# Side jobs of the input projection's pair stage, split into steps that are counted in matrix products

## The chip, the core and the metric

The kernel runs on one core of one Trainium2 chip. TensorE (PE in the profile, its weight loads PEld) multiplies; VectorE (DVE), ScalarE (ACT) and GpSimd (POOL) compute on SBUF and PSUM; SyncE (SP) issues most of the DMAs, and GpSimd issues some. Each engine works through its own queue in order. The metric is the time of one execution in device microseconds (us), the median of several runs.

## The reference

One inference step of a hybrid layer, in float32, for a prompt of 1024 rows and a sample of 64 rows with cached keys, values and states:

```python
xn = _rmsnorm(x, p['norm_mix_w'])
proj = xn @ p['w_in']                       # 1024 wide in, z | xBC | dt | q | k | v | g_ssm | g_att out
z, xbc, dt_raw, q, k, v, gate_ssm, gate_att = jnp.split(proj, ...)
...                                         # conv, SSD scan over chunks of 64, gated norm
q = _partial_rope(_rmsnorm(q.reshape(b, t, 2 * ATT_HEADS, ATT_HEAD_DIM), p['q_norm_w']), q_pos)
k = _partial_rope(_rmsnorm(k.reshape(b, t, 2 * ATT_HEADS, ATT_HEAD_DIM), p['k_norm_w']), q_pos)
k_all = jnp.concatenate([k_past, k], axis=1)
o = _diff_attention(q, k_all, v_all, q_pos, k_pos, lam)
...
x = x + mix @ p['w_out']
...                                         # conv feed-forward
return x, k, v, ssm_new, conv_new, ffn_new  # the normed and rotated k is an output
```

## The kernel before

**Arithmetic.** A float32 number is held as two parts: `hi`, the number rounded to a shorter format (a copy on ACT), and `lo`, the rest (a subtraction on DVE). A product of two numbers is three matmuls (hi x hi, hi x lo, lo x hi), summed in PSUM. The 1088 columns (1024 + 64 rows of the input) lie in the free dimension.

**Stages.** A first stage (up to about 56 us) computes the dt columns and value tiles of the projection, then come the other value tiles with their normalisation, the pair stage (about 116 to 489 us), the attention and the scan with the gate tiles and the rest of the projection (to about 1080 us), the output matrices and the feed-forward part.

**The pair stage.** It projects z, q and k in the manner of Winograd and Strassen: a block of 256 rows of output is seven products of sums of weights and sums of the input. There are 16 blocks n = 0 to 15: four of q, four of k, eight of z (`INPUT`). Each of the seven products p = 0 to 6 is done for two column halves s, so a block has 14 products, and each is 12 matmuls of 128 x 272 columns on line L584 (`pile` inside `in_pair`). A product's sum is evicted from its PSUM bank as soon as it stands: p = 0 and p = 2 by ACT (L619, L629), p = 1 and 3 by DVE (`u`, L621, L623), p = 4, 5 and 6 by DVE (`pre`, L631). p = 2 goes on in the bank of p = 0, p = 3 in that of p = 1 and p = 6 in that of p = 4, once these have been read. An eviction may therefore come about three products late before a matmul has to wait for it.

**What runs beside the products.**
- The weights of the next block: a load of `w_f` (SP), sums on POOL (L502, L503, L527, L531), `hi` on ACT (L479) and `lo` on DVE (L489).
- When a block is done, its rows are stored to DRAM: z through a SiLU to `z_sc`, q and k to `q_r` and `k_r` (L612), with their squares summed in `ss`.
- The side jobs, in the iterator `beside`: `steps()` (8 turns), `cached_keys()` (8 parts of the cached keys, split into `hi` and `lo` and stored to `c_st`), and, after the four q blocks are done, `finishing("q")` and `finishing("k")`. Each of these has four idle turns, three statistics, then 12 parts (a fetch of 128 x 544 from `q_r` or `k_r` on POOL's queue, L726; a scale on DVE, L730; for k a store of the result to the output `kT`, L717, which the trace calls `out_dram`; `hi` on ACT, L410; `lo` on DVE, L411, in the place of x; two stores to `q_st` or `k_st`, L721), and four rotated parts (two fetches L738 and L739, the second of the `rope` table; the scale L744; the rotation L748 to L751; then the same stores).

The fetch and the rest of a part lie one turn apart (`in_turn`: it prepares the next item and finishes the one before), and a turn is given after every third product:

```python
u.send((p, s))
if s == 1:
    more_left(n + 1)
if at % 3 == 0:
    next(beside, None)
```

What is still left after the last block is run out by `run(beside)`. `seen["read"]` and `seen["copy"]` are the last eviction on DVE and ACT; a step recorded inside `tc.issue_after(...)` is not placed ahead of it. A list scheduler then sets each engine's order. Before, the jobs need 73 turns and the blocks give 74.

**Buffers.** The x of all jobs come from `fx` (three buffers of 128 x 1088 columns), `xh`, the rope rows `rp` and the rotation's product `rt` from `fc` (three). Weights come from the pool `wp` with tiles of 1088 columns, of which all but those of the first stage use 1024 or fewer.

**After the pair stage** the scores of the attention (`sc`, L986) need `q`, `kh` and `kl`, loaded from `q_st` and `k_st` on SP's queue (L914), and the gate tiles are plain products on L161 to L163.

Of the kernel before, what the change touches and what calls it, by code (L numbers as in the profile page):

```python
# [9 lines left out]
F32 = mybir.dt.float32  # L10
# [7 lines left out]
P = 128  # L18
# [42 lines left out]
RAW = 6  # L61
IN_ROWS = dict(fs=2, fu=2, fp=3, fc=3, fx=3, ss=2)
ZS = 4
# [26 lines left out]
def hybrid_layer(ctx: ExitStack, tc: tile.TileContext, xT, xt, prm, cst, rope, wvd, win, wbs, wba, wout, wup, wdn,  # L90
# [45 lines left out]

    wp = tc.alloc_tile_pool(name="wp", bufs=1, side="right")
    extra, turn, ahead, quick = None, 0, AHEAD_IN, QUICK

    def weight_tiles(k, m, pool=None):  # L140
        nonlocal turn
        if pool is None:
            turn = (turn + 1) % 3
        p, b = (pool, 1) if pool is not None else (extra, 1) if extra is not None and turn == 0 else (wp, 2)
        w = p.tile([P, WMAX], F32, name="w_f", tag="w_f", bufs=b)
        hi = p.tile([P, WMAX], R32, name="w_hi", tag="w_hi", bufs=b)
        lo = p.tile([P, WMAX], R32, name="w_lo", tag="w_lo", bufs=b)
        return [t[:, : k * m].rearrange("p (k m) -> p k m", k=k) for t in (w, hi, lo)]
# [248 lines left out]
    for u in range(2):  # L397
        w = wp.tile([P, WMAX], F32, name="w_f", tag="w_f", bufs=2)[:, :1024]
# [93 lines left out]
    def left_parts(blocks, early=None, by=G, order=(0, 1, 2, 3)):  # L492

        a = []
        for src in blocks:
            w = wp.tile([P, WMAX], F32, name="w_f", tag="w_f", bufs=2)
# [14 lines left out]
        def shared():  # L511
            t = [wp.tile([P, WMAX], R32, name=x, tag=x, bufs=2) for x in ("w_hi", "w_lo")]
# [18 lines left out]
        by.tensor_tensor(out=s2, in0=q12, in1=s2, op=ALU.subtract)  # L531
        hi, lo = (wp.tile([P, WMAX], R32, name=x, tag=x, bufs=2)[:, :n] for x in ("w_hi", "w_lo"))
        split_left(hi, lo, s2)
# [164 lines left out]

    def finishing(kind):
# [13 lines left out]

        def put(x, hi, j, n, c, w):
            rows_at = lambda y, r0: y[r0 + P * j : r0 + P * (j + n), c : c + w].rearrange("(j p) t -> p j t", p=P)
            if keep is not None:
                load(out=rows_at(keep, 0), in_=x)  # L717
            lo = x.bitcast(R32)
            split(hi, lo, x)
            for u, y in enumerate((hi, lo)):  # L720
                load(out=rows_at(to, D * u), in_=y.bitcast(F32))  # L721

        def part_of(j, c):
            def prepare():
                x = row("fx", "x")
                G.dma_start(out=x, in_=d[P * j : P * (j + 1), c : c + HT])  # L726
                return x,

            def finish(x):
                V.scalar_tensor_tensor(x, x, wcol(j), rs[:, c : c + HT], ALU.mult, ALU.mult)  # L730
                put(x.unsqueeze(1), row("fc", "xh", R32)[:, :HT].unsqueeze(1), j, 1, c, HT)

            return prepare, finish

        def turned(c):
            def prepare():
# [5 lines left out]
            def finish(x, cosine):  # L742
                for j in range(2):
# [7 lines left out]
                V.tensor_tensor(out=x[:, 1], in0=x[:, 1], in1=y[:, 0], op=ALU.add)  # L751
                put(x, couple(t.bitcast(R32)), 0, 2, c, QW)

            return prepare, finish

        yield from in_turn([part_of(j, c) for j in range(2, KT) for c in (0, HT)])
        for c in range(0, T, QW):
            yield from in_turn([turned(c)])

    def cached_keys():  # L760
        def part_of(j):
            def prepare():
                x = row("fx", "x")[:, :PAST]
                G.dma_start(out=x, in_=ckT[P * j : P * (j + 1), :])
                return x,

            def finish(x):
                hi = row("fc", "xh", R32)[:, :PAST]
                split(hi, x.bitcast(R32), x)
                for u, y in enumerate((hi, x)):  # L770
                    load(out=c_st[D * u + P * j : D * u + P * (j + 1), :], in_=y.bitcast(F32))

            return prepare, finish

        yield from in_turn([part_of(j) for j in range(KT)])

# [30 lines left out]
    while len(left[1]) < 7:  # L807
        more_left(1)
    beside = chain(steps(), cached_keys())
# [550 lines left out]
    def kept_weights(block, at):  # L1360

        w = wp.tile([P, WMAX], F32, name="w_f", tag="w_f", bufs=2)[:, :1024]
# [468 lines left out]
```

## Time and profile before

| | |
|---|---|
| median of 3 runs | 2460.97 us (2459.64 to 2466.04) |
| profiled execution, its own time | 2462.09 us |
| its span | 2460.3 us |
| mean granted clock of TensorE | 0.995 |
| TensorE busy | 2399.9 us (98%) |
| VectorE busy | 1752.4 us (71%) |
| ScalarE busy | 1223.4 us (50%) |
| GpSimd busy | 691.8 us (28%) |
| the pair stage | 116.4 to 489 us |

The profile is of one execution. A row of the timeline gives the start, the length, the engine, the line of the kernel, the instruction with its output and inputs, how many of them, and in brackets how long the engine was idle before it and what ended that wait. A row of a wait table gives the waiting engine and line, what it waited for, the time in total, the number of times and the longest. The granted clock is the share of full speed that TensorE was given.

### The profile page before, as it was taken

The page shows a single profiled execution, that of the slowest core. Times are in us where ns is not written, and L with a number is a line of the kernel's source. Part 1 is how long each engine was busy: PE and PEld are TensorE (multiplying, and loading weights), DVE is VectorE, ACT ScalarE, POOL GpSimd, SP SyncE. Part 2 cuts the span into 40 slices and gives each one's busy share as a digit, 9 for nine tenths or more (in the row PEclk, how much of TensorE's full clock was granted, in tenths as well). Part 3 has the DMA queues.
Part 4 walks back from the last instruction along what each step waited for, and adds up shares of the span by engine and source line. Part 5 has one row for each costly group of instructions (what it writes and reads, how often), then busy time and mean ns, then how long its engine had stood idle before and what let it go on. Part 6 is the DMA issues. An engine that isn't in the chain of part 4 may idle for free. (4 is left out here: it accounts for less than half of the span.)

```text
span 2460.3 us, 49370 instructions
## 1 busy us (share of the span) xinstructions
PE 2399.9 (98%) x18744; PEld 2322.8 (94%) x18744; DVE 1752.4 (71%) x3113; ACT 1223.4 (50%) x2706; POOL 691.8 (28%) x758
## 2 busy tenths in 40 slices
PE   8999999899999999999999999999999999999998
PEld 8999999899999999998899998999999999999998
DVE  4596885758687786865877665756977777787763
ACT  7354445346566565656655554434533333343441
POOL 0023233201011010114533331012254554535433
PEclk9999999999999999999999999999999999999999
DMA  7855666874554444345897954764124234268784
GB/s 254 277 169 184 224 209 215 280 211 139 164 155 139 131 146 148 108 135 190 277 329 253 332 183 149 214 204 155 55 91 172 91 123 169 80 237 232 197 216 77
DMA packets 283089, 449.79 MB, mean 183 GB/s; under 512 B 35610, under 2 KB 189347, under 8 KB 282851
## 3 DMA queue, kind: packets, MB, share of 16 engines
q1 hardware_dynamic: 271810, 420.30, 52.2%
q0 software_dynamic: 11040, 26.34, 5.5%
q8 instruction: 147, 2.41, 0.4%
q14 instruction: 92, 0.75, 0.1%
HBM read 294.03 MB, written 152.50 MB: 181 GB/s over the span
## 5 line engine op out<-in xcount | busy, mean ns | idle before, releaser
L161 PE MATMUL mm<-b,w_hi 128*128 128x272 f32 x1792 | 529.5, 296 | 3.8 <-ACT gt L847 1.9
L163 PE MATMUL mm<-b,w_lo 128*128 128x272 f32 x1792 | 523.4, 292 | 1.3 <-DVE w_lo L155 1.1
L162 PE MATMUL mm<-b,w_hi 128*128 128x272 f32 x1792 | 522.1, 291 | 0.0
L161 PEld LDWEIGHTS mm<-b,w_hi 128*128 128x128 f32 x1792 | 338.6, 189 | 9.9 <-issue 4.2
L163 PEld LDWEIGHTS mm<-b,w_lo 128*128 128x128 f32 x1792 | 338.1, 189 | 4.7 <-issue 2.2
L162 PEld LDWEIGHTS mm<-b,w_hi 128*128 128x128 f32 x1792 | 338.8, 189 | 3.2 <-issue 2.3
L876 DVE SCALAR_TENSOR_TENSOR cc<-pre,par,cc 128x272 f32<-128x272 f32 (+1 forms) x288 | 140.0, 490 | 15.7 <-ACT cc L874 12.8
L1492 PE MATMUL mx<-m,w_hi 128*128 128x272 f32 x760 | 146.5, 290 | 3.0 <-DVE hb L1528 1.8
L1492 PE MATMUL mx<-n,wh 128*128 128x272 f32 x1080 | 144.2, 288 | 1.9 <-ACT wh L479 1.0
L155 DVE TENSOR_TENSOR w_lo<-w_f,w_hi 128x1024 fp32r<-128x1024 f32 (+1 forms) x82 | 103.3, 1262 | 55.8 <-ACT w_hi L154 53.6
L864 POOL COPY pre<-pre 128x3 f32<-128x3 f32 x72 | 23.5, 327 | 417.7 <-DVE cc L878 194.7
L1492 PEld LDWEIGHTS mx<-n,wh 128*128 128x128 f32 x1080 | 138.5, 188 | 2.5 <-ACT wh L479 1.2
L479 ACT CAST w_hi<-ws 128x512 fp32r<-128x512 f32 (+1 forms) x100 | 61.0, 610 | 158.3 <-PE mx L1492 76.8
L1000 ACT ACTIVATE p_t<-sc,mx 128x512 f32<-128x512 f32 (+6 forms) x144 | 106.2, 740 | 66.4 <-DVE mx L991 32.2
L483 DVE TENSOR_TENSOR wh<-w_f,wh 128x512 fp32r<-128x512 f32 (+1 forms) x101 | 99.1, 982 | 35.1 <-ACT wh L479 35.0
L1492 PEld LDWEIGHTS mx<-m,w_hi 128*128 128x128 f32 x760 | 119.4, 188 | 4.0 <-DVE hb L1528 2.4
L154 ACT CAST w_hi<-w_f 128x1024 fp32r<-128x1024 f32 (+1 forms) x82 | 85.9, 1048 | 69.6 <-PE mm L162 46.6
L1509 POOL TENSOR_TENSOR hb<-hb,cc 128x64 f32<-128x64 f32 (+2 forms) x66 | 86.4, 1328 | 110.7 <-DVE hb L1530 52.3
L502 POOL TENSOR_TENSOR ws<-w_f 128x512 f32<-128x512 f32 (+1 forms) x46 | 61.3, 1333 | 193.9 <-DMA w_f<-in_win_dram 114.2
L479 ACT CAST wh<-w_f 128x512 fp32r<-128x512 f32 (+1 forms) x144 | 88.1, 614 | 44.8 <-POOL pre L1523 15.4
L1492 PE MATMUL mx<-m,w_lo 128*128 128x272 f32 x380 | 109.8, 289 | 0.0
L1172 ACT ACTIVATE bc<-bc,nacum 128x128 f32<-128x128 f32 (+1 forms) x288 | 87.3, 383 | 15.7 <-POOL bc L1170 15.5
(452 smaller groups left out, 6974.8 us busy)
## 6 DMA issues: line engine op xcount, KB each, us to landing
w_f<-in_win_dram SPq DMA_DIRECT2D x78, 512.0 KB, 4.3
w_f<-in_wup_dram SPq DMA_DIRECT2D x45, 512.0 KB, 3.5
bc<-a_sc SPq DMA_DIRECT2D x32, 512.0 KB, 5.8
h_sc<-hb SPq DMA_DIRECT2D x44, 272.0 KB, 2.1
ht<-h_sc SPq DMA_DIRECT2D x22, 544.0 KB, 5.2
t_sc<-ht SPq DMA_DIRECT2D x22, 544.0 KB, 3.5
out_dram<-yq POOLq DMA_DIRECT2D x44, 272.0 KB, 5.8
x_sc<-cc SPq DMA_DIRECT2D x72, 136.0 KB, 2.4
```

The source lines that it names most:

```text
L154: S.copy(hi, w)
L155: V.tensor_tensor(out=lo, in0=w, in1=hi, op=ALU.subtract)
L161: PE.matmul(ps, a_hi, b_hi, start=i == 0, stop=False)
L162: PE.matmul(ps, a_hi, b_lo, start=False, stop=False)
L163: PE.matmul(ps, a_lo, b_hi, start=False, stop=i == n - 1)
L479: S.copy(hi, src)
L483: V.tensor_tensor(out=lo, in0=src, in1=hi, op=ALU.subtract)
L876: V.scalar_tensor_tensor(cc[:, :m], pre[:, i : i + m], cw(i), cc[:, :m], ALU.mult, ALU.add)
L1000: act(p_t[:n, :nk], sc[c][:n, :nk], AF.Exp, bias=mx[:n, c : c + 1], accum_out=dst)
L1172: act(bc[:L, e, :L], bc[:L, e, :L], AF.Exp, bias=nacum[:L, ch, 8 * g + e : 8 * g + e + 1])
L1492: PE.matmul(ps, w[x][:, c], b[y][:, k], start=start and k == i == 0, stop=k == 3 and i == 2, skip_group_check=not start)
L1509: G.tensor_tensor(out=hb[h][:, o : o + n], in0=hb[h][:, o : o + n], in1=cc[:, d : d + n], op=ALU.mult)
```

## The change

It touches the side jobs of the pair stage and two sizes.

- `in_turn` goes. A part is now a generator `job` in steps, and each step says how many products later the next one comes: fetch; 3 products; scale (and for k the store to `kT`); 1 product; `hi` on ACT and its store; 2 products, or 3 where there is a store to `kT`; `lo` on DVE and its store. `take_turn(at)` is called after every product, advances the jobs that run, and begins a new one after every third product.
- A rotated part takes one such start (before, two turns: the iterator of each held one item). The jobs now need 62 starts of the 74.
- `fx` has four buffers for x (before, three).
- The weight pool is closed after the first stage and opened again with tiles of 1024 columns (before, one pool of 1088).

```diff
-IN_ROWS = dict(fs=2, fu=2, fp=3, fc=3, fx=3, ss=2)
+IN_ROWS = dict(fs=2, fu=2, fp=3, fc=3, fx=4, ss=2)
...
+    wp.release()
+    wp, wide = tc.alloc_tile_pool(name="wp", bufs=1, side="right"), 4 * 256
...
-    def in_turn(items):
-
-        due = []
-        for prepare, finish in chain(items, [(None, None)]):
-            if prepare is not None:
-                due.append((finish, prepare()))
-            if len(due) > 1 or prepare is None and due:
-                finish, x = due.pop(0)
-                with tc.issue_after(seen["read"].ins):
-                    finish(*x)
-            yield
+    def job(fetch, scale, hi_of, hi_rows, lo_rows, keep=None):
+
+        x = fetch()
+        yield 3
+        hi = lambda: None
+        if scale is not None:
+            with after("read"):
+                x = scale(x)
+            if keep is not None:
+                load(out=keep, in_=x)
+            yield 1
+        with after("copy"):
+            hi = hi_of()
+            S.copy(hi, x)
+        load(out=hi_rows, in_=hi.bitcast(F32))
+        yield 2 if keep is None else 3
+        with after("read"):
+            V.tensor_tensor(out=x.bitcast(R32), in0=x, in1=hi, op=ALU.subtract)
+        load(out=lo_rows, in_=x)
+
+    running = []
+
+    def take_turn(at):
+        for x in list(running):
+            x[0] -= 1
+            if x[0] <= 0:
+                x[0] = next(x[1], None)
+                if x[0] is None:
+                    running.remove(x)
+        if at % 3 == 0:
+            new = next(beside, False)
+            if new:
+                running.append([next(new), new])
+            return new is not False or running
...
-            if at % 3 == 0:
-                next(beside, None)
+            take_turn(at)
...
-    run(beside)
+    while take_turn(0):
+        for _ in range(2):
+            take_turn(1)
```

The line numbers move: the products stand on L586, the evictions on L621, L623, L625, L631 and L633, the weights' `lo` on L491, the fetches of a part on L755, its scale on L759, its `kT` store on L708, `hi` and its store on L713, `lo` on L716 and its store on L717; a rotated part has its fetches on L771 and L772, its scale on L779 and the rotation on L783 to L786.

VectorE's queue, k parts beside the block that starts with `u_5137` (the numbers behind u mark the block): the scale, the subtraction and the evictions, before.

```order
L411 TENSOR_TENSOR x<-x,xh 128x544
L621 TENSOR_TENSOR u_5137<-mx,u_5136 128x272
L730 SCALAR_TENSOR_TENSOR x<-x,par,ss 128x544
L621 TENSOR_TENSOR u_5137<-mx,u_5136 128x272
L489 TENSOR_TENSOR wh<-w_f,wh 128x512
L730 SCALAR_TENSOR_TENSOR x<-x,par,ss 128x544
L411 TENSOR_TENSOR x<-x,xh 128x544
L623 TENSOR_TENSOR u_5136<-mx,u_5136 128x272
```

There the subtraction L411 of a part comes within an eviction or two of its scale L730. The same kind of place now, from the eviction of p = 3 on:

```order
L759 SCALAR_TENSOR_TENSOR x<-x,par,ss 128x544
L716 TENSOR_TENSOR x<-x,xh 128x544
L625 TENSOR_TENSOR u_4911<-mx,u_4911 128x272
L491 TENSOR_TENSOR wh<-ws_4948,wh 128x512
L625 TENSOR_TENSOR u_4911<-mx,u_4911 128x272
L491 TENSOR_TENSOR wh<-w_f,wh 128x512
L716 TENSOR_TENSOR x<-x,xh 128x544
L633 TENSOR_TENSOR pre<-mx,u_4911 128x272
L759 SCALAR_TENSOR_TENSOR x<-x,par,ss 128x544
```

The L716 directly behind an L759 belongs to the part before; the part of that L759 is subtracted at the next L716, behind two evictions and two weight splits.

VectorE's queue at the q rotations, now: from the second eviction of p = 3 (`u`) on, behind the scale of the first rotation.

```order
L625 TENSOR_TENSOR u_3801<-mx,u_3801 128x272
L491 TENSOR_TENSOR wh<-w_f,wh 128x512
L783 TENSOR_TENSOR rt<-x,rp 128x544
L633 TENSOR_TENSOR pre<-mm,u_3801 128x272
L784 TENSOR_TENSOR x<-x,rp 128x544
L633 TENSOR_TENSOR pre<-mm,u_3801 128x272
L491 TENSOR_TENSOR wh<-w_f,wh 128x512
L779 SCALAR_TENSOR_TENSOR x<-x,wq_1552,ss 128x272 x2
L785 TENSOR_TENSOR x<-x,rt 128x272
L786 TENSOR_TENSOR x<-x,rt 128x272
L633 TENSOR_TENSOR pre<-mx,u_3801 128x272
L783 TENSOR_TENSOR rt<-x,rp 128x544
```

Before, the same block has the beginning of one rotation, between the evictions of p = 6:

```order
L631 TENSOR_TENSOR pre<-mm,u_3791 128x272 x2
L489 TENSOR_TENSOR wh<-w_f,wh 128x512
L631 TENSOR_TENSOR pre<-mx,u_3791 128x272 x2
L489 TENSOR_TENSOR w_lo<-ws_3833,w_hi 128x512
L631 TENSOR_TENSOR pre<-mm,u_3792 128x272
L744 SCALAR_TENSOR_TENSOR x<-x,wq_1548,ss 128x272 x2
L748 TENSOR_TENSOR rt<-x,rp 128x544
L631 TENSOR_TENSOR pre<-mm,u_3792 128x272
```

The rotations of q begin earlier in the block and stand closer.

TensorE's queue at the end of the pair stage, before:

```order
L584 MATMUL mm<-b_1598,w_hi 128x272
L584 MATMUL mm<-b_1597,w_lo 128x272
L986 MATMUL sc<-kh_6145,q_6143 128x512
L986 MATMUL sc<-kh_6145,q_6143 128x128
L161 MATMUL mm<-b_916,w_hi 128x272
```

and now, the last product's end and, 48 matmuls of L161 to L163 later, the first scores:

```order
L586 MATMUL mm<-b_1602,w_hi 128x272
L586 MATMUL mm<-b_1601,w_lo 128x272
L161 MATMUL mm<-b_920,w_hi 128x272
L162 MATMUL mm<-b_921,w_hi 128x272
L163 MATMUL mm<-b_920,w_lo 128x272
```

```order
L161 MATMUL mm<-b_926,w_hi 128x272
L162 MATMUL mm<-b_927,w_hi 128x272
L163 MATMUL mm<-b_926,w_lo 128x272
L1021 MATMUL sc<-kh_6149,q_6147 128x512
L1022 MATMUL sc<-kl_6152,q_6147 128x512
```

Two products of a gate tile have moved ahead of the first scores.

More of the change, by code (lines that the diff above doesn't have):

```diff
@@ L511, in shared @@
         def shared():
-            t = [wp.tile([P, WMAX], R32, name=x, tag=x, bufs=2) for x in ("w_hi", "w_lo")]
+            t = [wp.tile([P, wide], R32, name=x, tag=x, bufs=2) for x in ("w_hi", "w_lo")]
             for i, src in enumerate((s1, q22)):
@@ L531, in left_parts @@
         by.tensor_tensor(out=s2, in0=q12, in1=s2, op=ALU.subtract)
-        hi, lo = (wp.tile([P, WMAX], R32, name=x, tag=x, bufs=2)[:, :n] for x in ("w_hi", "w_lo"))
+        hi, lo = (wp.tile([P, wide], R32, name=x, tag=x, bufs=2)[:, :n] for x in ("w_hi", "w_lo"))
         split_left(hi, lo, s2)
@@ L712, in finishing, with rows_at, part, fetch @@
             yield
[L714 to L724, printed above, removed]
+        def rows_at(y, r0, j, n, c, w):
+            return y[r0 + P * j : r0 + P * (j + n), c : c + w].rearrange("(j p) t -> p j t", p=P)
+        def part(j, c):
+            def fetch():
                 x = row("fx", "x")
                 G.dma_start(out=x, in_=d[P * j : P * (j + 1), c : c + HT])
[L727 to L729 removed]
+                return x
+            def scale(x):
                 V.scalar_tensor_tensor(x, x, wcol(j), rs[:, c : c + HT], ALU.mult, ALU.mult)
[L731 to L733 removed]
+                return x.unsqueeze(1)
+            at = j, 1, c, HT
+            return job(fetch, scale, lambda: row("fc", "xh", R32)[:, :HT].unsqueeze(1), rows_at(to, 0, *at), rows_at(to, D, *at),
+                       None if keep is None else rows_at(keep, 0, *at))
         def turned(c):
[L736 removed]
+            t = None
+            def fetch():
                 x, cosine = couple(row("fx", "x")), couple(row("fc", "rp"))
@@ L751, in finish, with part, fetch @@
                 V.tensor_tensor(out=x[:, 1], in0=x[:, 1], in1=y[:, 0], op=ALU.add)
-                put(x, couple(t.bitcast(R32)), 0, 2, c, QW)
-            return prepare, finish
-        yield from in_turn([part_of(j, c) for j in range(2, KT) for c in (0, HT)])
+                return x
+            at = 0, 2, c, QW
+            return job(fetch, scale, lambda: couple(t.bitcast(R32)), rows_at(to, 0, *at), rows_at(to, D, *at),
+                       None if keep is None else rows_at(keep, 0, *at))
+        for j in range(2, KT):
+            for c in (0, HT):
+                yield part(j, c)
         for c in range(0, T, QW):
-            yield from in_turn([turned(c)])
+            yield turned(c)
     def cached_keys():
-        def part_of(j):
-            def prepare():
+        def part(j):
+            def fetch():
                 x = row("fx", "x")[:, :PAST]
                 G.dma_start(out=x, in_=ckT[P * j : P * (j + 1), :])
[L765 to L775, printed above, removed]
+                return x
+            return job(fetch, None, lambda: row("fc", "xh", R32)[:, :PAST], *(c_st[D * u + P * j : D * u + P * (j + 1), :] for u in range(2)))
+        for j in range(KT):
+            yield part(j)
     def begun_in(n):
@@ L808, in hybrid_layer @@
         more_left(1)
-    beside = chain(steps(), cached_keys())
+    beside = chain(one_by_one(steps()), cached_keys())
     for n in range(1, len(INPUT)):
```

26 lines of the change are left out of this document (18 added, 8 removed).

## The prediction

> **What bounds the kernel now.** I read the page first, then the busy time by windows, the engine's own waits, and TensorE's timeline where it has a gap. The page says that TensorE is nearly the whole of the time:
>
> ```profile
> span 2460.3 us, 49370 instructions
> PE 2399.9 (98%) x18744; PEld 2322.8 (94%) x18744; DVE 1752.4 (71%) x3113; ACT 1223.4 (50%) x2706; POOL 691.8 (28%) x758
> ```
>
> Only 2460.3 - 2399.9 = 60 us are idle on PE. A change that leaves the matmuls alone can win part of that, and what PE loses by running at a lower clock. By windows (after each pair of times: length, PE busy; the number behind the POOL column is PE's granted clock, then the DMA share):
>
> ```profile
> 400.00:489.00 89.00, 78.16 (x596) 76.48 (x594) 62.79 (x106) 36.41 (x66) 26.02 (x28) 0.98 0.83 275
> 520.00:1080.00 560.00, 560.00 (x4317) 538.41 (x4316) 435.54 (x1028) 349.88 (x944) 57.17 (x163) 1.00 0.47 141
> ```
>
> The 560 us after the pair stage have no idle at all. The stretch 400 to 489, where the k parts run beside the products, has 89.00 - 78.16 = 10.8 us. TensorE's timeline shows the gaps (start, length, instruction, and in brackets the idle time before it with its releaser). The first two rows here are undisturbed: one starts 3.01 us after the other, so 12 matmuls, one product, take 1.505 us.
>
> ```profile
> 298.65 3.18 PE L584 MATMUL mx<-b,wh 128*128 128x272 f32 x24
> 301.66 3.19 PE L584 MATMUL mx<-t,wh 128*128 128x272 f32 x24
> 306.88 4.80 PE L584 MATMUL mx<-b,wh 128*128 128x272 f32 x24 [2.03 <-ACT u L619]
> ...
> 402.05 1.78 PE L584 MATMUL mx<-t,wh 128*128 128x272 f32 x12 [1.13 <-DVE u L621]
> 411.17 0.52 PE L584 MATMUL mx<-b,w_hi 128*128 128x272 f32 x2 [1.30 <-DVE pre L631]
> 426.27 1.77 PE L584 MATMUL mx<-t,wh 128*128 128x272 f32 x12 [1.20 <-DVE u L621]
> 435.69 0.52 PE L584 MATMUL mx<-b,w_hi 128*128 128x272 f32 x2 [1.60 <-DVE pre L631]
> 481.62 0.82 PE L584 MATMUL mm<-b,w_hi 128*128 128x272 f32 x2 [2.27 <-DVE pre L631]
> 489.11 0.87 PE L986 MATMUL sc<-kh,q 128*128 128x512 f32 x2 [2.80 <-ACT w_hi L154]
> 490.38 0.56 PE L161 MATMUL mm<-b,w_hi 128*128 128x272 f32 x1 [0.40 <-DVE pre L631]
> 494.14 0.43 PE L162 MATMUL mm<-b,w_hi 128*128 128x272 f32 x1
> 494.37 0.43 PE L163 MATMUL mm<-b,w_lo 128*128 128x272 f32 x1
> ```
>
> In each of these PE waits for an eviction of a product sum, so the question is what held the evicting engine. VectorE's waits answer it (in order: total us, times, longest):
>
> ```profile
> DVE x L411 <- DMA out_dram<-x: 16.8, 10, 3.8
> DVE x L730 <- DMA x<-k_r: 7.8, 4, 2.8
> ```
>
> The largest is self-made. For a k part the scaled x is stored to the output (out_dram), and the subtraction that overwrites x (L411) stands right behind in VectorE's queue, so VectorE sits until the store has read x. The eviction L621 stands behind that in its queue, and PE's gap at 402.05 ends with it:
>
> ```profile
> 399.83 1.82 DVE L411 TENSOR_TENSOR x<-x,xh 128x544 fp32r<-128x544 f32 x1 [3.84 <-DMA out_dram<-x]
> ```
>
> **The change, part by part.** *The k parts.* The subtraction now comes 1 + 3 = 4 products after the scale, 4 x 1.505 = 6.0 us. The store takes
>
> ```profile
> out_dram<-x SPq DMA_DIRECT2D x16, 272.0 KB, 3.7
> x<-k_r POOLq DMA_DIRECT2D x16, 272.0 KB, 4.3
> ```
>
> 3.7 us from issue, so it is covered with 2.3 us over. The gaps at 402.05, 411.17 and 435.69 (1.13 + 1.30 + 1.60 = 4.0 us) go whole. The wait for x<-k_r does not go: a part is still fetched three products, 4.5 us, ahead, a fetch takes 4.3 us, and it is issued from POOL's queue behind the weight sums. The fourth x buffer only lets that issue be punctual. I leave half of the gap at 426.27 in place: 0.6 of 1.20 us goes. The last gap, 2.27 us at 481.62, stands where the last rotations ran into the last block; the new steps end about two blocks earlier, so it goes, with its slow matmuls of the next 3 us (13 of them at about 0.23 us, the spacing of the last two rows, instead of 0.125: 1.3 us). I take 0.6 us off for what comes in its place. Sum: -4.0 - 0.6 - 2.3 - 1.3 + 0.6 = -7.6; I use -7.5.
>
> *The end of the stage.* Before, the last rotations of k lie in the last block, and their stores stand in SP's queue before and among the loads of the scores, the next user of TensorE:
>
> ```profile
> 483.55 1.54 SPq L914 DMA_DIRECT2D kh<-k_st  x2
> ```
>
> The scores' loads were issued at 483.55 to 485.09, and PE, which had nothing else in its queue, stood until 489.11: 2.80 + 0.40 = 3.2 us. Behind it about 26 matmuls ran at 494.37 - 494.14 = 0.23 instead of 0.125 us, 2.6 us more. Now PE has two products of a gate tile (48 matmuls, 6.0 us) before the first score, which covers the 4 us that the loads took, and no k store is left in the queue. Of 5.8 us I take -5.0; 0.8 stays for the first gate matmul, which may wait for an eviction (0.40 before).
>
> [...] The gaps of 2.03, 2.27 and 2.80 us were each followed by slow matmuls (24 in 4.80 us at 306.88, against 3.18), those of 1.1 to 1.6 us by none. So I count a clock cost for gaps of over 2 us, here 1.3 + 2.6, and 1.6 for 306.88. [...]
>
> *Cached keys and q parts.* The cached keys have one gap, and the q parts a second one beside that at 306.88:
>
> ```profile
> 218.58 1.77 PE L584 MATMUL mm<-b,wh 128*128 128x272 f32 x12 [1.26 <-ACT u L619]
> 295.52 0.51 PE L584 MATMUL mx<-b,w_hi 128*128 128x272 f32 x2 [0.70 <-DVE pre L631]
> ```
>
> ACT stood there for a key fetch that POOL issued late, behind a store from the third buffer; with four it should be earlier: -1.0 of 1.26. The q parts have no kept store; theirs are the gaps of 0.70 and 2.03 with the slow 24 matmuls (1.6 us), in all 4.3. They come with POOL's sums and with fetches that wait for a buffer. I count -3.0.
>
> *The rotated parts* are the new load. One takes on VectorE:
>
> ```profile
> 486.22 0.91 DVE L744 SCALAR_TENSOR_TENSOR x<-x,par,ss 128x272 f32<-128x272 f32 x2 [3.95 <-DMA x<-k_r]
> 488.03 0.71 DVE L748 TENSOR_TENSOR rt<-x,rp 128x544 f32<-128x544 f32 x1
> 490.15 0.71 DVE L749 TENSOR_TENSOR x<-x,rp 128x544 f32<-128x544 f32 x1
> 492.62 0.43 DVE L751 TENSOR_TENSOR x<-x,rt 128x272 f32<-128x272 f32 x1
> 496.10 0.72 DVE L411 TENSOR_TENSOR x<-x,rt 128x544 fp32r<-128x544 f32 x1 [3.05 <-DMA out_dram<-x]
> ```
>
> 0.91 + 0.71 + 0.71 + 0.43 + 0.43 + 0.72 = 3.9 us (L750 and L751 are alike). It had six products (9.0 us) and now has three (4.5 us). Evictions and weight splits (six in a block of 14 products) go beside it:
>
> ```profile
> 465.49 0.43 DVE L631 TENSOR_TENSOR pre<-mm,u 128x272 f32<-128x272 f32 x1
> 465.84 0.68 DVE L489 TENSOR_TENSOR w_lo<-w_f,w_hi 128x512 fp32r<-128x512 f32 x1
> ```
>
> Five of seven products are evicted by VectorE: 3 x 5/7 x 0.43 = 0.9 us, and 3 x 6/14 x 0.68 = 0.9 us of splits in three products: 5.7 us of work in 4.5, so VectorE falls 1.2 us behind per turn and 4.7 us in four. An eviction may be three products, 4.5 us, late before PE waits for its bank. So four bare rotations just fit; a fetch that lands late does not. I take +2.0 for the q rotations (bounds 0 and the 2.27 of one gap plus 2.03 of another, 4.3), and nothing for the k rotations beyond the 0.6 above.
>
> *The early stage.* Since the weight pool is closed and opened again after the first stage, the loads of the third and fourth value tiles wait for that stage's last product (55.8 us), and were free to go at 31.55 us. They are needed three value products later:
>
> ```profile
> 55.78 0.29 PE L161 MATMUL mx<-w_hi,xn_hi 128*128 128x272 f32 x1
> 64.83 0.28 PE L161 MATMUL mm<-w_hi,xn_hi 128*128 128x256 f32 x1
> 56.40 1.03 ACT L154 CAST w_hi<-w_f 128x1024 fp32r<-128x1024 f32 x1
> 57.47 1.23 DVE L155 TENSOR_TENSOR w_lo<-w_f,w_hi 128x1024 fp32r<-128x1024 f32 x1 [0.55 <-ACT w_hi L154]
> w_f<-in_win_dram SPq DMA_DIRECT2D x78, 512.0 KB, 4.3
> ```
>
> 64.83 - 55.78 = 9.05 us of cover against 4.3 + 1.03 + 1.23 = 6.6 us for one and about 1 more for the second: 0 if the loads go at once, up to 3 if they queue. I take +0.5. The narrower tiles change no instruction's size. In the other 1940 us only neighbours swap in the order; I allow 4 us either way and count 0.
>
> Sum: -7.5 - 5.0 - 1.0 - 3.0 + 2.0 + 0.5 = -14.0. The profiled execution took 2462.09 us (span 2460.3 and 1.8 around it), 1.1 above the median of 2460.97. 2460.97 - 14 = **2447 us**. A measurement of this kernel can tell about 0.3%, 7.4 us, from no change.
>
> **The rivals.**
> 1. *The stalls move.* VectorE waits 7.8 us for x<-k_r at L730, and the lead of the fetch is unchanged; what the subtraction no longer waits for, the scale might. For it: 4.3 us landing against 4.5 of lead. Against: the largest gaps followed the store's wait. Then only the end's idle time is won (-3 to -5), less the rotations (+2): about -3, 2458.
> 2. *Slower: the crowded rotations.* Place: the eight turns with a rotation. The slack left is nil after four bare ones, so it decides when VectorE waits over 3.3 us in a turn (4.5 - 1.2); it did wait 3.95 for x<-k_r at 486.22 and PE lost 2.27. Neighbours of POOL's sums are longer as well:
>
> ```profile
> 262.50 3.68 DVE L730 SCALAR_TENSOR_TENSOR x<-x,wq,ss 128x544 f32<-128x544 f32 x1
> 263.05 1.29 POOL L503 TENSOR_TENSOR ws<-ws,w_f 128x512 f32<-128x512 f32 x1
> 403.25 0.77 DVE L730 SCALAR_TENSOR_TENSOR x<-x,par,ss 128x544 f32<-128x544 f32 x1
> ```
>
> 3.68 beside POOL's sums, 0.77 without. If every turn loses 2.27 (18 us) and half of them the clock (4 x 1.5 = 6), that is +24 in place of the +2.0, and the sum is -16 + 24 = +8: 2469. Against it: the block of 14 products, 21.1 us, has room for 10 evictions (4.3), six splits (4.1) and the 2.7 rotations that fall into it (10.5), together 18.9. [...]
> 3. *The early gap.* If the reloads queue behind one another, PE loses 3 us and 2 of clock: 2447 + 5 = 2452.
> 4. *All of it goes.* No rotation cost and all gaps with their clock (7.5 + 1.3, 5.8, 1.3, 4.3): -20, 2441.
>
> **How the numbers follow.** Forecast 0.55, stalls move 0.17, slower 0.15, early gap 0.06, all goes 0.07. The range leaves out most of the slower case and a little below: 2440 to 2463. Faster by over 0.3%: the forecast, all goes and the early gap, less 0.01 for the forecast's own tail (its range is 2442 to 2455), 0.67; same: the stalls that move and that tail, 0.18; slower 0.15.
>
> **What would show it.** Right: no wait of VectorE's subtraction for out_dram above 1 us; the 400-to-489 stretch some 7 us shorter; gate matmuls directly after the last product and no gap before the first score; the k stores over two blocks before the end. Wrong: gaps of over 2 us in blocks with rotations, waits on rp<-in_rope_dram or x<-k_r longer than 3.3 us, a gap near 64.8 us, or a busy sum of PE that differs by more than the clock explains.

## The result and the profile after

The changed kernel takes 2455.86 us (median of 10 runs, 2448.28 to 2458.71) against 2463.07 us before (median of 10, 2458.10 to 2466.04). The ratio is 0.9971, 95% interval 0.9959 to 0.9982: 7.2 us faster. The forecast was 14 us faster; the sign was right, the size half. The profiled execution took 2457.46 us, 1.6 above its median, so the two traces differ by only 4.6 of the 7.2 us:

```profile
span 2455.7 us, 49366 instructions
PE 2398.2 (98%) x18744; PEld 2323.0 (95%) x18744; DVE 1738.6 (71%) x3113; ACT 1225.4 (50%) x2707; POOL 694.8 (28%) x758
```

TensorE's timeline, all gaps of over 1 us from the pair stage to 520 us (start, length, instruction, idle time before it and its releaser):

```profile
125.96 0.52 PE L586 MATMUL mx<-b,w_hi 128*128 128x272 f32 x2 [2.70 <-ACT u L621]
150.50 0.52 PE L586 MATMUL mm<-t,w_hi 128*128 128x272 f32 x2 [1.32 <-DVE pre L633]
296.43 0.52 PE L586 MATMUL mx<-b,w_hi 128*128 128x272 f32 x2 [1.31 <-DVE pre L633]
320.84 0.52 PE L586 MATMUL mm<-b,w_hi 128*128 128x272 f32 x2 [2.97 <-DVE pre L633]
345.46 0.51 PE L586 MATMUL mm<-b,w_hi 128*128 128x272 f32 x2 [2.82 <-DVE pre L633]
393.86 0.59 PE L586 MATMUL mx<-b,w_hi 128*128 128x272 f32 x2 [2.01 <-DVE pre L633]
427.65 2.58 PE L586 MATMUL mm<-b,wh 128*128 128x272 f32 x12 [1.79 <-ACT u L621]
515.42 0.44 PE L1021 MATMUL sc<-kh,q 128*128 128x384 f32 x1 [2.56 <-ACT p_t L1035]
```

The gap of 1.26 us at the cached keys and the 3.2 us ahead of the first scores are gone, and the five k gaps of before have become two. New are 2.97 and 2.82 us beside the q rotations, 1.9 us more at the start, and 2.56 us at 515, behind the gate products that were moved forward. The points at which the two traces can be laid side by side are the fifth product (123.55 before, 125.96 after), the last matmul of the pair stage (486.0 and 487.0) and the last score, whose start ends the ranges here, before and then after:

```profile
L986 PE MATMUL sc<-kh,q x208: 191/338/765, 489.1 to 1073.1; 128*128 128x512 f32 x73, 128*128 128x384 f32 x8, 128*128 128x256 f32 x8, 128*64 128x64 f32 x8
```

```profile
L1021 PE MATMUL sc<-kh,q x208: 191/338/506, 493.2 to 1070.6; 128*128 128x512 f32 x73, 128*128 128x384 f32 x8, 128*128 128x256 f32 x8, 128*64 128x64 f32 x8
```

So the start lost 2.4 us, the rest of the pair stage won 1.4 (362.4 to 361.0), the end of the stage won 3.5 (587.1 to 583.6), and the stretch behind it won 2.1 (1387.2 to 1385.1), a stretch that takes 1381.5 to 1392.0 us in the traces of all the kernels here. VectorE's waits of the side jobs over the stage:

```profile
DVE x L759 <- DMA x<-k_r: 9.8, 3, 4.2
DVE x L716 <- DMA out_dram<-x: 7.7, 7, 1.7
DVE x L759 <- DMA x<-q_r: 5.3, 3, 2.9
DVE rt L783 <- DMA rp<-in_rope_dram: 2.2, 2, 1.6
```

The wait for the kT store, 16.8 us before, is 7.7, none longer than 1.7. The wait of the scale for fetched k rows, 7.8 us before, is 9.8. One of them in VectorE's timeline, and POOL's queue ahead of an earlier one of 3.54 us (at 391.09):

```profile
424.63 0.78 DVE L759 SCALAR_TENSOR_TENSOR x<-x,par,ss 128x544 f32<-128x544 f32 x1 [4.21 <-DMA x<-k_r]
```

```profile
382.05 1.50 POOL L504 TENSOR_TENSOR ws<-w_f 128x512 f32<-128x512 f32 x1 [10.66 <-DMA w_f<-in_win_dram]
383.63 1.28 POOL L505 TENSOR_TENSOR ws<-ws,w_f 128x512 f32<-128x512 f32 x1
384.87 1.77 POOL L529 TENSOR_TENSOR w_f<-w_f 128x512 f32<-128x512 f32 x1
386.59 1.09 POOL L755 DMA_DIRECT2D x<-k_r  x2
```

Two fetches that were due at different times left together at 386.6, behind three sums that had waited for their weights; one of them is the row that VectorE then waited 3.54 us for, ahead of TensorE's gap at 393.86. The row of 424.63, ahead of the gap at 427.65, came late for another reason. Its fetch, the last of the k parts, stood on POOL until a store had left its buffer:

```profile
417.82 0.55 POOL L755 DMA_DIRECT2D x<-k_r  x1 [3.56 <-DMA k_st<-x]
```

POOL stood so ahead of k fetches for 13.1 us in all, although there are four buffers. POOL's whole work in this stage is such sums, all on SBUF tiles (56, busy 79.5 us from 116 to 488 us), and 48 DMA issues; the sums in PSUM are evicted by VectorE (160 evictions) and ACT (64) alone.

### The profile page after: what moved, and what is told of

It reads as the page before. It is cut to its first block, busy times and chain, and to the rows that moved or that the text cites. A ratio compares the mean times of both kernels' runs of the same rounds, so it can differ in the third digit from the quotient of the medians.

```text
span 2455.7 us, 49366 instructions
## 1 busy us (share of the span) xinstructions
PE 2398.2 (98%) x18744; PEld 2323.0 (95%) x18744; DVE 1738.6 (71%) x3113; ACT 1225.4 (50%) x2707; POOL 694.8 (28%) x758
## 4 chain that ended last, share of the span: by engine, by line
PE 65%; DMA 7%; DVE 5%; issue 2%; POOL 1%; ACT 1%; SPq 1%; DVEq 0%; POOLq 0%; ACTq 0%
PE mx L1527 10%; PE mm L161 8%; PE mm L163 8%; PE mm L162 8%; PE mm L1527 4%; PE mx L1685 4%; PE po L1070 3%; PE mm L1685 2%; PE mx L161 2%; PE sc L1022 2%; PE sc L1021 2%; PE mx L163 2%; PE mx L162 2%; PE pt L1050 2%; PE yi L1216 1%
## 5 line engine op out<-in xcount | busy, mean ns | idle before, releaser
L161 PE MATMUL mm<-b,w_hi 128*128 128x272 f32 x1792 | 529.4, 295 | 1.2 <-DVE b_g L229 1.2
L163 PE MATMUL mm<-b,w_lo 128*128 128x272 f32 x1792 | 523.4, 292 | 1.4 <-DVE w_lo L155 1.3
L161 PEld LDWEIGHTS mm<-b,w_hi 128*128 128x128 f32 x1792 | 338.1, 189 | 7.4 <-issue 3.8
L163 PEld LDWEIGHTS mm<-b,w_lo 128*128 128x128 f32 x1792 | 337.7, 189 | 3.4 <-DVE w_lo L155 2.0
```

What stands on the lines that cost most here:

```text
L161: PE.matmul(ps, a_hi, b_hi, start=i == 0, stop=False)
L163: PE.matmul(ps, a_lo, b_hi, start=False, stop=i == n - 1)
```

## The experiments

The theory from these traces was that the steps and the early end gained what the trace shows, and that the re-opened pool (start) and the crowded rotations took it back. The main rival: what gains is the fourth x buffer, and the steps are worth nothing.

Each ratio is the time over that of the kernel before, run beside it. The kernel before took 2462.9 to 2468.2 us in these comparisons, so different experiments are compared by their ratios and not by their times. In the code of the edits, three dots stand for further lines.

**1. The re-opened pool alone, on the kernel before.** Edit, as in the change:

```diff
...
+    wp.release()
+    wp, wide = tc.alloc_tile_pool(name="wp", bufs=1, side="right"), 4 * 256
...
```

> The kernel before with one part of the change alone: the weight pool closed after the first stage and opened again with 1024 columns (three x buffers and the old turns stay). Theory: the value tiles' late loads push the start of the pair stage back, as in the changed kernel (gap before the fifth product 2.70 us in place of 0.84, stage start 0.5 us later): 2 to 3 us slower than before, about 2465.5. Rival: the reload is hidden and the late start has another cause: within 0.5 us of before.

Ratio 0.9992 (0.9981 to 1.0003). The gap at the start is there, 3.22 us, but the kernel is not slower, or by no more than the 0.7 us that the interval allows: the fifth product comes 1.25 us later (124.80), and from there to the last score it takes 949.6 us, as before (949.55). The theory's 2 to 3 us are not in the time.

**2. The steps without the size edits**, from the changed kernel:

```diff
-IN_ROWS = dict(fs=2, fu=2, fp=3, fc=3, fx=4, ss=2)
+IN_ROWS = dict(fs=2, fu=2, fp=3, fc=3, fx=3, ss=2)
...
-    wp.release()
-    wp, wide = tc.alloc_tile_pool(name="wp", bufs=1, side="right"), 4 * 256
```

> The changed kernel without the two size edits: one weight pool of 1088 columns, three x buffers. Theory (the pool costs 2.3 us, the fourth buffer matters little): 2453.5, gap at the stage's start back to 0.8 us. Rival (the fourth buffer carries the gain in the k parts, since a fetch waits for a store out of its buffer): 2459 or more, with VectorE waiting longer for x<-k_r.

Ratio 0.9989 (0.9976 to 1.0002), 2459.59 us: the rival. Without the two size edits most of the gain is gone, and by experiment 1 the pool is not what gave it.

**3. Rotated parts in two turns again, in the changed kernel.**

```diff
         for c in range(0, T, QW):
             yield turned(c)
+            yield iter((1,))
```

> The changed kernel with an idle turn behind each rotated part, as before the change (70 of 74 turns used). Theory that crowded rotations eat the gain: the gaps of 2.97 and 2.82 us beside the q rotations fall below 1 us each, 5 us faster than the changed kernel, about 2451, of which the later end of the k jobs may take 2 back. Rival (those gaps come from POOL's sums, whatever the spacing): gaps of 2 to 3 us remain, time within 1 us of the changed kernel.

Ratio 0.9958 (0.9942 to 0.9973), 2453.09 us. The gaps beside the q rotations shrink from 2.97 and 2.82 to 1.29 and 0.56 us, as expected of crowding, while a gap of 2.79 us appears at 376.27, at a statistic of k. The time is 3 us better than the changed kernel by the ratios, but the two intervals overlap.

**4. Fetches on SyncE's queue, in the changed kernel.**

```diff
-                G.dma_start(out=x, in_=...)
+                load(out=x, in_=...)
...
```

`load` issues on SyncE's queue; the fetches of the rope rows and of the cached keys move with it.

> The changed kernel with the fetches of x and the rope rows issued on SyncE's queue in place of POOL's. Theory that a fetch comes late because POOL issues it behind up to three weight sums (1.29 us each), and that sums come late behind a fetch that waits for its buffer: the VectorE waits of 3.5 and 4.2 us for x<-k_r go, and the late weight casts with them: 5 us faster than the changed kernel, about 2451. Rival: SyncE's stores, which wait for computed rows, hold the fetches as long as POOL's sums did: no gain, or up to 5 us slower.

Ratio 0.9948 (0.9931 to 0.9966), 2449.19 us, the lowest ratio of all that ran, though its interval overlaps that of the changed kernel. VectorE's waits for fetched k rows fall from 9.8 to 3.7 us:

```profile
DVE x L759 <- DMA x<-k_r: 2.5, 3, 1.7
DVE x L779 <- DMA x<-k_r: 1.2, 1, 1.2
```

So POOL's queue does hold part of the fetches up. What that is worth is not shown: from the fifth product to the last score this trace takes 944.1 us, the changed kernel's 944.6. A k gap of 2.81 us is left at 419.85, and the q gaps remain (2.70, 1.59, 2.82 us), so these are another matter.

**5. Both of these together**, in the changed kernel:

```diff
-                G.dma_start(out=x, in_=...)
+                load(out=x, in_=...)
...
             yield turned(c)
+            yield iter((1,))
```

> The changed kernel with both edits that made it faster: fetches on SyncE's queue, and an idle turn behind each rotated part. Theory that the two remove different delays (fetch late behind POOL's sums; VectorE overfull in rotation turns): the gains of 2.8 and 6.7 us add to some 8, about 2447.5. Rival that both cure one thing, the q gaps: no better than the SyncE fetches alone, 2449 to 2450.

Ratio 0.9966 (0.9953 to 0.9978), 2454.02 us. They do not add; it is no better than either. Differences of 2 to 5 us among kernels with four buffers are no more than these intervals can tell, so 3 to 5 are not ranked against each other or the changed kernel here.

**6. The subtraction two products behind the scale, in place of four.**

```diff
-        yield 2 if keep is None else 3
+        yield 2 if keep is None else 1
```

> The changed kernel with the k parts' subtraction two products behind the scale in place of four. Theory that the distance to the kT store is what the steps give the k parts: VectorE's waits for out_dram at the subtraction go from 7.7 us in 7 to over 14 us, the kernel 3 to 4 us slower than the changed one, about 2459.5. Rival (the store's wait was cover for the late fetch, and what is not waited for one is waited for the other): within 1 us of the changed kernel.

Ratio 0.9966 (0.9953 to 0.9979), 2455.39 us: the same as the changed kernel, as the rival said. The wait for the store grew from 7.7 to 12.3 us, and the wait of the scale for fetched k rows fell from 9.8 to 1.1:

```profile
DVE x L716 <- DMA out_dram<-x: 12.3, 10, 2.6
DVE x L759 <- DMA x<-k_r: 1.1, 1, 1.1
```

What is not waited for the one is waited for the other. So the distance to the store is not worth the 3 to 4 us of the theory, but the run does not show that the store's wait costs nothing. One gap of TensorE ends with an eviction right behind such a wait:

```profile
406.49 0.72 DVE L716 TENSOR_TENSOR x<-x,xh 128x544 fp32r<-128x544 f32 x1 [1.75 <-DMA out_dram<-x]
407.62 3.29 PE L586 MATMUL mx<-t,wh 128*128 128x272 f32 x24 [0.80 <-DVE u L623]
```

**7. The size edits alone, with the old turns**, on the kernel before:

```diff
-IN_ROWS = dict(fs=2, fu=2, fp=3, fc=3, fx=3, ss=2)
+IN_ROWS = dict(fs=2, fu=2, fp=3, fc=3, fx=4, ss=2)
...
+    wp.release()
+    wp, wide = tc.alloc_tile_pool(name="wp", bufs=1, side="right"), 4 * 256
...
```

> The kernel before, with its old turns, and both size edits: four x buffers and the re-opened weight pool. Theory that steps and buffer work only together (the steps hold each x longer, so three buffers make the fetch wait): as the re-opened pool alone, 2461. Rival that the fourth buffer brings the gain by itself: 2457 or less.

Ratio 0.9960 (0.9947 to 0.9974), 2453.73 us. The whole gain, without a single step of the change. Beside experiment 1, which differs by the fourth buffer alone, VectorE's waits are, with three buffers,

```profile
DVE x L413 <- DMA out_dram<-x: 15.1, 8, 3.4
DVE x L732 <- DMA x<-k_r: 9.2, 5, 3.1
DVE x L732 <- DMA x<-q_r: 6.8, 2, 3.5
DVE x L746 <- DMA x<-k_r: 4.6, 2, 3.5
DVE rt L750 <- DMA rp<-in_rope_dram: 4.2, 2, 2.3
```

and with four:

```profile
DVE x L413 <- DMA out_dram<-x: 16.9, 11, 3.8
DVE x L732 <- DMA x<-q_r: 1.5, 2, 0.8
DVE x L732 <- DMA x<-k_r: 1.4, 2, 0.7
DVE rt L750 <- DMA rp<-in_rope_dram: 0.9, 1, 0.9
```

The waits for fetches fall from 24.8 to 3.8 us, the wait for the store stays. POOL's timeline shows why. With three buffers a k fetch stands until the last store has read its buffer (three rows of the run with three; the run with four has no such row for k):

```profile
436.81 0.56 POOL L728 DMA_DIRECT2D x<-k_r  x1 [1.66 <-DMA k_st<-x]
440.77 0.54 POOL L728 DMA_DIRECT2D x<-k_r  x1 [3.41 <-DMA k_st<-x]
466.25 0.72 POOL L740 DMA_DIRECT2D x<-k_r  x1 [5.19 <-DMA k_st<-x]
```

Of the twelve k fetches the seventh leaves at 420.53 with three buffers and at 411.98 with four, the last at 449.01 and at 436.40. With three, the scale of the seventh row and TensorE behind it stand:

```profile
426.38 0.78 DVE L732 SCALAR_TENSOR_TENSOR x<-x,par,ss 128x544 f32<-128x544 f32 x1 [3.13 <-DMA x<-k_r]
427.57 1.76 PE L586 MATMUL mx<-t,wh 128*128 128x272 f32 x12 [1.14 <-DVE u L623]
```

With four that scale waits 0.69 us, and TensorE has no gap between 402.52 and 433.49.

From the fifth product to the last score the run with four takes 941.9 us (127.05 to 1068.9), that with three 949.6: 7.7 us, which is the difference of the ratios (0.9992 - 0.9960 = 0.0032, 7.9 us). Of the 7.7 us, 6.4 are idle time of TensorE (21.13 to 14.75). What is left of the store's wait still costs something with four buffers:

```profile
400.27 1.84 DVE L413 TENSOR_TENSOR x<-x,xh 128x544 fp32r<-128x544 f32 x1 [3.76 <-DMA out_dram<-x]
402.52 1.77 PE L586 MATMUL mx<-t,wh 128*128 128x272 f32 x12 [1.14 <-DVE u L623]
```

**8. Fetches on SyncE's queue in the kernel before.**

```diff
-                G.dma_start(out=x, in_=...)
+                load(out=x, in_=...)
...
```

> The kernel before with the fetches on SyncE's queue, nothing else. Theory that POOL's order (fetch behind weight sums, sums behind a waiting fetch) costs as much there: 5 us faster than before, 2458. Rival that SyncE's queue, which there holds stores that wait for the late subtraction, gives it back: within 1 us of before.

Ratio 1.0000 (0.9986 to 1.0015). With three buffers another queue gains nothing: the fetch waits for its buffer there too (at the parts' fetches SyncE's queue stands 28.2 us for `q_st<-x` and 7.3 us for `k_st<-x`).

**9. The changed kernel with three buffers**, the pool re-opened:

```diff
-IN_ROWS = dict(fs=2, fu=2, fp=3, fc=3, fx=4, ss=2)
+IN_ROWS = dict(fs=2, fu=2, fp=3, fc=3, fx=3, ss=2)
```

> The changed kernel with three x buffers, the steps and the re-opened pool kept. Theory that the fourth buffer carries the whole gain, steps or not: 2460 to 2463, no faster than the re-opened pool alone (0.9992). Rival that the steps have a gain of their own beside the buffer: 2457 or less.

Ratio 1.0010 (0.9995 to 1.0024). The steps hold each x longer (3 + 1 + 3 products and two stores), so with three buffers VectorE waits still more for fetched rows,

```profile
DVE x L759 <- DMA x<-k_r: 14.6, 6, 4.2
DVE x L716 <- DMA out_dram<-x: 12.4, 7, 3.6
DVE x L759 <- DMA x<-q_r: 8.7, 3, 5.2
```

and PE has a gap longer than any that another run has in the stage:

```profile
294.31 5.42 PE L586 MATMUL mx<-t,wh 128*128 128x272 f32 x24 [5.39 <-DVE u L623]
```

The profiled execution took 2482.01 us, 11.7 above the median of this kernel, so these rows overstate its usual run.

**10. The size edits and an early end, with the old turns.** Two of the four idle turns ahead of q's and k's jobs are left out, and the order then has the two gate products ahead of the first scores, as in the change:

```diff
-        for _ in range(4):
+        for _ in range(2):
             yield
```

> The kernel before with both size edits, and two of the four idle turns ahead of q's and k's jobs left out: 69 turns of 74, so that no k store is left among the scores' loads and two gate products come before the first scores, as in the changed kernel. Theory that the end of the stage is worth the 3 to 5 us that the gap there shows, on top of the buffer: 2449 to 2450, no gap before the first scores. Rival that PE's work moved ahead is only missing later: within 1 us of the sizes alone, 2454.

Ratio 0.9952 (0.9935 to 0.9969) against 0.9960 without: 2 us, within the intervals. The gap ahead of the first scores is gone, which experiment 7 still has:

```profile
487.20 0.87 PE L988 MATMUL sc<-kh,q 128*128 128x512 f32 x2 [3.16 <-DMA kh<-k_st]
```

**11. The scale five products behind the fetch, in the changed kernel.**

```diff
         x = fetch()
-        yield 3
+        yield 5
```

> The changed kernel with the scale five products behind the fetch in place of three. Theory that the waits for x<-k_r (9.8 us in 3, up to 4.2) and x<-q_r cost PE the gaps of 2.0 and 1.8 us beside the k parts: they go, 3 to 4 us faster than the changed kernel, 2452. Rival that each x is then held 11 products, nearly as long as four buffers allow, so fetches wait for a buffer as they did with three: 2459 or slower.

Ratio 0.9963 (0.9946 to 0.9980): 2 us better by the middle, not separable from the changed kernel. The waits for x<-k_r do not go (9.7 us at the scale): each x is now held 5 + 1 + 3 products and two stores, and a fetch still waits for its buffer (POOL stands 7.58 us for `k_st<-x` ahead of the one at 416.54). Whether a longer lead gains with a fifth buffer was not tried.

**12. The early end alone, on the kernel before** (the edit of 10).

> The kernel before, three buffers and the old pool, with two of the four idle turns left out (69 turns). The end of the stage alone: 5 us by the prediction's term, so 2458. Rival as in the run with the sizes: within 1 us of before, 2462 to 2463.

Ratio 0.9993 (0.9980 to 1.0007): at most 5 us, most likely under 2. The gap before the first scores is gone in this trace, and a new one stands where the changed kernel has it too:

```profile
525.79 0.44 PE L986 MATMUL sc<-kh,q 128*128 128x384 f32 x1 [2.37 <-ACT p_t L1000]
```

The reading is that the gate products that covered this wait for the softmax have been used up earlier. All twelve kernels with the early end have a gap there, 1.43 to 3.00 us in ten of them and 0.5 us in experiments 10 and 11; in the other five no score waits more than 0.25 us for the softmax.

**13. What the fourth buffer frees.** Each statistic of q and k takes two x buffers. Here one of the two rows gets a tile of its own, with three buffers and the re-opened pool:

```diff
-            t = [row("fx", "n1") for _ in range(2)]
+            t = [row("fx", "n1"), rows_r.tile([P, 384], F32, name="n1", tag="fn", bufs=1)]
```

> The kernel before with the re-opened pool and three x buffers, and one of the two rows that each statistic takes out of them moved to a tile of its own (384 columns). While a statistic runs, two buffers are left for x, as with four buffers; otherwise three. Theory that the parts' fetches need the fourth buffer (a fetch waits until the last store has left its buffer): as the re-opened pool alone, 0.999. Rival that the statistics' hold is what the fourth buffer pays for: 0.996.

Ratio 0.9993 (0.9983 to 1.0003), as the pool alone, and VectorE's waits for fetched rows stay at 24.1 us. So it is not the statistics that need the fourth buffer; the fetches of the parts are left.

**14. and 15. Other addresses for the first rows**, in the changed kernel and in that of experiment 10:

```diff
+    row("fc", "sq")
     four = row("ss", "st")
```

> The changed kernel with one of the rows used late (fc) allocated first, so that the rows lie at other addresses. Theory that the 2.70 us gap at the start is the first eviction's row lying on a value row whose store lands late: the gap falls below 1 us, and the kernel is 2 us faster, 0.9963. Rival that the late store is only a sign of a later value stage: the gap stays, 0.9971.

> The old turns with both size edits and two idle turns left out (0.9952 before), with the rows placed as in the run beside it. If the start gap goes with the placement, 2 us faster, 0.9944; else the same.

Ratios 0.9958 (0.9945 to 0.9971) and 0.9964 (0.9949 to 0.9978). The gap at the start stays, 3.26 and 3.68 us. In 14 ACT's first eviction still ends a wait of 7.98 us for the last value store (out_dram<-vo); in 15 it ends one of 7.90 us that the trace puts down to another transfer (t<-p_t). The edit did not take the wait away, so why the first eviction waits so long stays open.

Over all, the ten kernels with four x buffers lie between 0.9948 and 0.9971, the six with three between 0.9989 and 1.0010, whatever else they do. All ten have the re-opened pool as well; four buffers beside the old pool were not run.

## Why the prediction was right or wrong

**What bounds the kernel:** right. PE's sum hardly changed (2399.9 and 2398.2 us); what moved is its idle time and clock in the pair stage and just behind it.

**The k parts, -7.5: the step that failed.** The prediction let the gaps at 402, 411 and 435 go with the wait for the kT store, and left the wait for fetched rows half of one gap. In the trace before, the store's waits do stand ahead of the gaps at 402 and 411 (3.84 and 3.42 us; gaps of 1.13 and 1.30). Ahead of the gap at 435 VectorE waits 1.11 us for a k row and only 0.20 us for the store, and the one at 481 comes behind a wait of 2.08 us for rope rows. So 2.4 us of gaps belong to the store, and the other large ones stand behind fetches.

The change did lower the store's wait to 7.7 us, but fetches that came late took its place: both large k gaps of the changed kernel stand behind waits for k rows, of 3.54 and 4.21 us. Nor does the time follow the store's wait: kernels with 16.9, 12.3 and 7.7 us of it (experiments 7 and 6 and the changed kernel) have ratios of 0.9960, 0.9966 and 0.9971. This is rival 1, the stalls move.

In the trace the k gaps became 2.01 + 1.79 + 0.18 = 4.0 us in place of 7.5 (8.1 with the one of 0.64), but each of the two large ones was followed by slow matmuls (24 in 4.64 us in place of 3.02, some 1.6 us lost at each), where before only the last was (1.3): 2 us won, not 7.5. One trace is a coarse measure of this: experiment 14, the same kernel with other addresses, has 7.0 us of gaps there. The prediction's own signs also spoke: waits for the store of up to 1.7 us (it asked for none above 1), waits for x<-k_r longer than 3.3 us, and gaps of over 2 us beside rotations.

**The fourth buffer** was priced at "lets that issue be punctual", within the 0.6 us, and 1.0 us at the cached keys. It carries the whole gain: 7.7 us between experiments 1 and 7. Rival 1 had the right row (x<-k_r, 7.8 us) and the wrong conclusion from it, that the fetch's lead is unchanged: the lead in products is, but a fetch that stands for its buffer has less, and the prediction's own price for a full lead, 4.3 us landing against 4.5, left no room for that. The steps then use up part of what the buffer gives, since they hold each x longer: POOL stands 13.1 us for k_st<-x ahead of k fetches in the changed kernel, and not at all in experiment 7.

**The end of the stage, -5.0.** The mechanism came true: two gate products ahead of the first scores, no gap there, and the last k store goes out at 464.0 us in place of 496.9, about one block ahead of the end and not two (the range of starts is ahead of the semicolon):

```profile
L717 SPq DMA_DIRECT2D k_st<-x x16: 319/371/479, 378.2 to 464.0; - x16
```

In the trace it is worth 3.5 us, since 2.56 us came back at 515. Alone, in the kernel before, it is 0.9993 and not distinguishable from nothing (experiment 12). The term was too large because it asked only what the moved products cover at the new place, not what they had covered at the old one. It also counted about 26 slow matmuls; the rows show some 20 gate matmuls 0.23 us apart, 490.4 to 495.0, some 2 us in place of 2.6.

**Cached keys, -1.0:** right in size, since the gap of 1.26 us is gone, but not for the reason given. With three buffers and the old turns it is gone as well in the traces of experiments 1 and 13.

**q parts and rotations, -3.0 + 2.0:** wrong by 5. The gaps there went from 3.05 to 7.10 us. With four buffers the crowding of the rotations shows in every trace: beside the q rotations TensorE's gaps sum to 4.3 to 5.8 us in the five kernels with a rotation in each turn (the changed one, 4, 6, 11, 14) and to 0.2 to 1.9 us in the five with two turns for each (3, 5, 7, 10, 15); with three buffers the two kinds overlap (1.7 and 5.9 against 0.3 to 5.3). This agrees with the overload of 1.2 us a turn that the prediction worked out, so rival 2's mechanism was at work. Crowding is not all of it: ahead of the gap of 2.82 us VectorE also waits 1.60 us for rope rows, and three of its rows take 1.50, 1.81 and 1.50 us beside POOL's sums, where such rows take 0.72, 0.71 and 0.43 without. The rotations of k, whose blocks follow the part fetches, show no gap over 0.2 us in the changed kernel.

**The early stage, +0.5:** the first product of the pair stage is 0.5 us later (117.0 against 116.5), but that is no test of the term: it starts at 115.3 to 117.6 us in the kernels with the re-opened pool and at 116.2 to 117.4 in the others. What was missed is the first eviction, which then waits longer (7.37 us in place of 5.90, both put down to the last value store): the gap grows by 1.9 us in this trace, in every kernel with the re-opened pool the gap is 2.7 us or more, in the others 0.8 to 1.4. That it costs the total nothing in experiment 1 is measured, not explained.

**The clock.** The prediction counted slow matmuls behind any gap of over 2 us. The trace after does not bear this out (windows: length, PE busy and count; behind the POOL column the granted clock). Behind the gaps of 2.70 and 2.97 us:

```profile
125.90:129.00 3.10, 3.04 (x24) 3.04 (x25) 2.92 (x5) 2.39 (x7) 1.30 (x2) 1.00 1.14 352
320.80:323.00 2.20, 2.16 (x17) 2.16 (x18) 2.20 (x5) 1.20 (x3) 0.23 (x1) 1.00 0.97 269
```

and behind those of 2.82 and 1.79:

```profile
347.00:350.00 3.00, 3.00 (x12) 2.39 (x12) 1.66 (x4) 2.97 (x6) 0.00 (x0) 0.54 0.99 348
430.00:433.00 3.00, 3.00 (x20) 3.00 (x19) 2.93 (x6) 0.86 (x3) 0.45 (x1) 0.72 0.99 326
```

The longest gap left the clock at 1.00, a shorter one took it to 0.72. Gaps of 1.79 and 2.82 us were enough for a lower clock here and those of 2.70 and 2.97 us were not, so the limit of 2 us was the author's estimate from the gaps of the trace before; what decides it is not shown.

**The range and the sign** held (2440 to 2463), but not by the sum that gave them. The k parts and the q parts with their rotations each came out some 5 us worse than forecast, and the buffer that carries the gain had been priced at little.

## What to carry to other kernels

A wait that is large in the table of waits need not set the time: follow each single wait to the gap behind it, and ask which wait takes its place when it is gone. When software pipelining is stretched in time, count first how long each buffer is then held; here one more buffer gained all, and the longer steps without it gained nothing or less. Work that is moved forward to cover one gap can leave another uncovered, so price both places.

## What the runs showed of the hardware

Two things had not been expected. The granted clock behind a gap does not follow the gap's length (2.97 us left it at 1.00, 1.79 us took it to 0.72), so the slow stretches of a trace can't be counted from its gaps; one cost some 1.6 us here (behind the gap at 393.86 the clock was 0.55 from 393.80 to 397.50, the matmuls stand 0.23 us apart until 397.2, and 24 take 4.64 us in place of 3.02). And the stretch behind the last score, which none of the edits meant to touch, takes 1381.5 to 1392.0 us in the traces of the sixteen kernels and the kernel before. That makes the span of a single trace a poor measure of a change of 7 us: here the two traces differ by 4.6.
